# Four early feature tiles ahead of h2's sums, the sums on VectorE, and features loaded into their own tiles

## The chip, the cores and the metric

One Trainium2 chip, one of its cores. The metric is the device time of one launch of the program, in microseconds (us). A time is quoted as the median of several runs; the profile is one execution more.

## The reference, cut to what matters

One layer of a decoder (attention and gated mixers, then a convolutional feed-forward) for 1024 prompt rows and 8 samples of 4 rows, 1056 rows in all, width 1024. What the change touches is the second half:

```python
D_FF = ((8 * D_MODEL // 3) + 127) // 128 * 128        # 2816 = 22 * 128
# ConvFFN: up = (RMSNorm(x)*(1+scale2)+shift2) @ w_up; causal depthwise conv (width 3); gelu(a) * b; @ w_down
# x = x + gate2 * ffn
# Final RMSNorm.
```

`w_up` is 1024 by 5632, so `up` has 44 feature tiles of 128: 22 for `a` and 22 for the gate `b`. All data are fp32.

## The kernel before, in words

Activations lie transposed: partitions are features, columns are the 1056 rows. Every fp32 matmul is made of three: a tensor is split into `hi` (a cast by ScalarE, line 307) and `lo` (the rest, a subtraction by VectorE, line 308), and `mm` (line 56) multiplies hi by hi, hi by lo and lo by hi. A framework orders each engine's queue when the program is built; tags of the buffer pools and explicit calls of `issue_after` bound it.

**The output projection** writes `x1` in three column chunks (`CH`: 384, 384 and 288 columns). `h2`, the normalised and modulated `x1`, is made chunk by chunk behind it (`h2_tile`: a multiplication on VectorE in line 1373, an activation on ScalarE, and for the 32 sample columns a multiplication and an addition, lines 302 and 303, on the engine given by `eng`). The last chunk's are made after the projection has ended.

**The up projection** takes `a` and gate of one feature tile together, a pair, 22 times. A pair is one step of Strassen's scheme in Winograd's form over halves of the 1024 inputs and halves of the rows (`HR` = 528 columns, worked in two `HB` = 264): seven products, each of 24 matmuls of 264 columns. Two of them, `w11` by `BS[0:4]` and `a12` by `BS[4:8]`, need only plain pieces of `h2` from its first 528 columns; the other five need sums of `h2`: `F` (lines 1566 and 1567), `b2 - b1` (1572, on GpSimd), line 1575, each then turned into hi and lo (`turned`: ScalarE in 1555, VectorE in 1556, of which two on GpSimd). They need sums of weights as well, made by GpSimd in lines 1481 to 1484. `first_products` runs the two plain products of pairs 0 and 1 early, while the last chunk of `h2` is made; its result is added into the pair's `up` tile by line 1469. A pair ends with the convolution (ScalarE 1453, VectorE 1454 and 1455), gelu (1537), a multiplication on GpSimd (1538, 1540), and a store of the feature tile to `ff_d` in DRAM (1541). 

**The down projection** goes over the three column chunks again. In the first chunk three outputs run abreast, four features at a time, since the features come back from DRAM as they are needed: `ff_pair` (1603) loads two of them with one transfer into a buffer with the tag "raw", and splits them into their own tiles; `down_weights` loads and splits `w_down` (`weights`, line 1298) through the same three buffers. All weights of the second half of the kernel pass through these "raw" buffers of 128 by 1024. `late` (1591) writes one element of a raw buffer from the last pair's weights until the third output has its first weights, so that the first loads wait for that pair. GpSimd's queue loads `x1` back meanwhile (1663).

The lines that the change touches most:

```python
        raw = late(W([128, 1024], F32, "raw", 3))[:, 0:K * 128]
    ...
            t = slot(F32R) if (k < 6, 6 <= k < 16, k < 6)[c] else R6([128, 768], F32R, "ff", 22)
            split(raw[:, i * w:i * w + w], t[:, 0:w], t[:, 384:384 + w])
```

## Time and profile before

| what | us |
| --- | --- |
| median of 3 runs | 2070.89 (2068.14 to 2075.97) |
| the profiled execution | 2063.98 |
| its span | 2062.3 |
| TensorE busy | 1929.0 (94%) |
| VectorE busy | 1175.0 (57%) |
| ScalarE busy | 811.5 (39%) |
| GpSimd busy | 555.2 (27%) |

The span is what the profile shows from the first to the last instruction; 1.7 us of the execution lie around it. Busy shares are means over the whole span. TensorE idles little, so what a change may bring is found at the places where it idles: in the page's slices, around 1285 to 1345 us (where the up projection begins) and 1755 to 1820 us (where the down projection begins).

### The profile page before, as it was taken

Reading aid. Unit: us, or ns where it says so; the run is one execution under the profiler, and the core shown is the slowest. Engines: PE = TensorE matmul, PEld = TensorE weight load, DVE = VectorE, ACT = ScalarE, POOL = GpSimd, SP = SyncE. Lnnn points to the kernel's source line nnn. Section 1 sums busy time; section 2 is a strip of 40 time slices with the busy share of each in tenths; the row PEclk is TensorE's granted clock in tenths of the full one; section 3 lists DMA queues with packets and bytes.
Section 4 is the critical chain, followed back from the end, with each engine's and each line's share of the span. In section 5 each row is a group of like instructions: output and inputs, shape, how many; then the busy total and the mean of one; then the engine's idle time right before and its main releaser. Section 6 shows DMA issues by size and latency. Waiting matters only on the chain. (4 is left out here: it accounts for less than half of the span.)

```text
span 2062.3 us, 43509 instructions
## 1 busy us (share of the span) xinstructions
PE 1929.0 (94%) x15977; PEld 1748.4 (85%) x15977; DVE 1175.0 (57%) x2697; ACT 811.5 (39%) x1732; POOL 555.2 (27%) x668
## 2 busy tenths in 40 slices
PE   4999999999997999999999999799999999899996
PEld 3899899999995656666679999699999999789986
DVE  6512510121117756667674767988888888555554
ACT  3411211222214645456552355444444444354442
POOL 3310010100001212313320512766565655201010
PEclk7999999999997999999899999899999999999998
DMA  8465577654457666676652645133322222665553
GB/s 313 150 212 161 179 224 248 207 165 158 153 186 223 209 192 207 192 260 181 219 177 89 225 160 174 42 105 104 106 83 85 78 80 84 214 215 185 164 188 97
DMA packets 233620, 345.05 MB, mean 167 GB/s; under 512 B 32544, under 2 KB 183872, under 8 KB 231232
## 3 DMA queue, kind: packets, MB, share of 16 engines
q1 hardware_dynamic: 167008, 245.06, 36.8%
q10 hardware_dynamic: 55312, 58.01, 8.9%
q0 software_dynamic: 11088, 39.21, 5.3%
q8 instruction: 126, 2.06, 0.4%
q14 instruction: 86, 0.70, 0.1%
HBM read 304.91 MB, written 41.43 MB: 168 GB/s over the span
## 5 line engine op out<-in xcount | busy, mean ns | idle before, releaser
L56 PE MATMUL t<-t,t 128*128 128x264 f32 (+10 forms) x15266 | 1848.0, 309 | 96.4 <-ACT t L307 15.5
L56 PEld LDWEIGHTS t<-t,t 128*128 128x128 f32 (+3 forms) x15138 | 1667.3, 170 | 228.4 <-issue 87.3
L308 DVE TENSOR_TENSOR t<-t,t 128x512 fp32r<-128x512 f32 (+5 forms) x544 | 392.8, 736 | 335.1 <-ACT t L307 292.7
L307 ACT CAST t<-t 128x512 fp32r<-128x512 f32 (+5 forms) x544 | 310.4, 588 | 498.0 <-PE t L56 348.0
L1164 POOL TENSOR_SCALAR t<-t,t 128x384 f32<-128x384 f32 (+3 forms) x96 | 119.0, 1253 | 326.9 <-DVE t L1158 100.1
L1139 DVE TENSOR_REDUCE t<-t 128x1 f32<-128x384 f32 (+3 forms) x192 | 96.0, 517 | 56.4 <-PE t L56 55.6
L1513 DVE TENSOR_TENSOR t<-t,t 128x264 f32<-128x264 f32 (+2 forms) x370 | 112.5, 343 | 26.5 <-PE t L56 13.9
L1140 ACT ACTIVATE t<-t,t 128x384 f32<-128x384 f32 (+3 forms) x192 | 105.4, 554 | 54.9 <-DVE t L1139 35.2
L1179 ACT COPY t<-t 128x512 f32<-128x512 f32 (+1 forms) x136 | 76.4, 573 | 65.2 <-PE t L1176 48.9
L1176 PE MATMUL t<-t,t 128*128 128x128 f32 x528 | 87.5, 288 | 0.5 <-ACT t L1179 0.4
L1176 PEld LDWEIGHTS t<-t,t 128*128 128x128 f32 x528 | 57.8, 143 | 24.8 <-issue 23.2
L1624 POOL TENSOR_TENSOR t<-t,t 128x384 f32<-128x384 f32 (+1 forms) x12 | 14.9, 1271 | 234.6 <-ACT t L1681 234.6
L672 ACT ACTIVATE t<-t 128x384 f32<-128x384 f32 (+1 forms) x48 | 22.2, 464 | 136.4 <-PE t L56 105.4
L1454 DVE SCALAR_TENSOR_TENSOR t<-t,t,t 128x1072 f32<-128x1072 f32 x44 | 59.4, 1351 | 17.8 <-ACT t L1453 17.4
L1453 ACT ACTIVATE t<-t,t 128x1072 f32<-128x1072 f32 x44 | 56.6, 1285 | 24.6 <-DVE t L1513 15.5
L674 POOL DMA_DIRECT2D t<-t x16 | 8.5, 532 | 209.5 <-DVE t L673 178.4
L1538 POOL TENSOR_TENSOR t<-t,t 128x1024 f32<-128x1024 f32 x22 | 59.1, 2688 | 15.8 <-ACT t L1537 15.8
L1455 DVE SCALAR_TENSOR_TENSOR t<-t,t,t 128x1072 f32<-128x1072 f32 x44 | 59.3, 1347 | 0.1
L1481 POOL TENSOR_TENSOR t<-t 128x512 f32<-128x512 f32 x22 | 31.6, 1436 | 101.5 <-DMA t<-w_up 63.7
L1329 POOL TENSOR_TENSOR t<-t,t 128x384 f32<-128x384 f32 (+1 forms) x24 | 28.3, 1183 | 96.4 <-DMA t<-t 81.5
L699 POOL TENSOR_TENSOR t<-t,t 128x512 f32<-128x512 f32 (+1 forms) x12 | 11.9, 1002 | 151.6 <-DVE t L690 115.7
L1164 DVE TENSOR_SCALAR t<-t,t 128x384 f32<-128x384 f32 (+3 forms) x96 | 49.8, 571 | 0.9
(280 smaller groups left out, 1166.3 us busy)
## 6 DMA issues: line engine op xcount, KB each, us to landing
t<-psel SPq DMA_DIRECT2D x384, 128.0 KB
t<-pcmp SPq DMA_DIRECT2D x332, 128.0 KB
t<-t POOLq DMA_DIRECT2D x50, 528.0 KB, 4.0
t<-w_up SPq DMA_DIRECT2D x46, 512.0 KB
t<-pcmp ACTq DMA_DIRECT2D x180, 128.0 KB
t<-w_down SPq DMA_DIRECT2D x42, 512.0 KB
t<-psel ACTq DMA_DIRECT2D x128, 128.0 KB
t<-w_ada SPq DMA_DIRECT2D x16, 1024.0 KB
```

The lines of the kernel that those rows point to most:

```text
L56: return pe.matmul(out, lhsT, rhs, start=start, stop=stop)
L307: act.copy(hi, t)
L308: dve.tensor_tensor(lo, t, hi.bitcast(F32), op=OP.subtract)
L1139: dve.tensor_reduce(nm, bk, axis=AX.X, op=OP.max, negate=True)
L1140: act.activation(P[:, w:w + n], bk, AF.Exp, bias=nm, accum_out=s8[:, branch, h, c:c + 1])
L1164: (dve if e == "d" else pool).tensor_scalar(P, P, fc, None, op0=OP.mult)
L1176: pe.transpose(pt[:, 256 * a + 128 * h:256 * a + 128 * h + 128], P[:, c:c + 128], ident)
L1179: act.copy(pp[:, 0:n], pt[:, 0:n])
L1454: dve.scalar_tensor_tensor(acc[:, 0:w], up[:, 1:1 + w], cw[:, n, 1:2], acc[:, 0:w], op0=OP.mult, op1=OP.add)
L1455: dve.scalar_tensor_tensor(acc[:, 0:w], up[:, 2:2 + w], cw[:, n, 2:3], acc[:, 0:w], op0=OP.mult, op1=OP.add)
L1513: dve.tensor_tensor(o, by4(banks[c][:, c0:c0 + n], n), other(c, c0, n) if other else o, op=OP.add)
L1538: pool.tensor_tensor(a[:, 0:NP], a[:, 0:NP], g[:, 0:NP], op=OP.mult)
```

## The change

Four parts.

1. The raw buffers become six of 128 by 512 in place of three of 128 by 1024, each filled by its own transfer of 256 KB, in place of 512 KB.
2. `first_products` runs for four pairs in place of two, in program order between the sums of `h2`. It no longer adds its two products: ScalarE copies both into one tile, and the pair adds them when it starts (line 1499 of the changed kernel). The split of the weights of tiles 2 and 3 comes in here. Pair 0's sums of weights go to other buffers and come after the four.
3. All sums of `h2` are on VectorE: the sample columns, two of the subtractions in `turned`, and `b2 - b1` leave GpSimd.
4. Each feature of the down projection is loaded by its own transfer of 192 KB, for chunks of 384 columns, straight into the `lo` half of the tile that it will have, and split there, through no raw buffer; so three outputs abreast share the raw buffers with nothing. Two pools hold these tiles in place of one (16 and 6 buffers). The condition of `late` is now `not ff[0]`, and as features are asked for before weights, it never holds: no load waits for the last pair any more.

```diff
+    def raw_load(src, late=lambda t: t):
+        t = late(W([128, 512], F32, "raw", 6))[:, 0:src.shape[1]]
+        sync.dma_start(t, src)
+        return t
+
     def weights(src, K, late=lambda t: t):
-        raw = late(W([128, 1024], F32, "raw", 3))[:, 0:K * 128]
-        sync.dma_start(raw, src)
         w = [], []
         for k in range(0, K, 4):
-            hi, lo = parts(raw[:, 128 * k:128 * min(k + 4, K)])
+            hi, lo = parts(raw_load(src[:, 128 * k:128 * min(k + 4, K)], late))
...
     def first_products(j, behind=()):
 
-        up = up_tile()
-        p1 = slot()[:, 0:2 * HB]
-        X = [pA(), pA()]
-        half_products([t[0:4] for t in early[j]], BS[0:4], X, behind[0:1])
-        for c in range(2):
-            act.copy(p1[:, HB * c:HB * c + HB], X[c][:, 0:HB])
-        X = [pU(), pU()]
-        half_products([t[4:8] for t in early[j]], BS[4:8], X, behind[1:])
-        for o, c, c0, n in pieces(up, 0):
-            dve.tensor_tensor(o, X[c][:, c0:c0 + n], p1[:, HB * c:HB * c + n], op=OP.add)
-        return up, p1
+        t = slot()
+        for i, bank in enumerate((pA, pU)):
+            X = [bank(), bank()]
+            half_products([w[4 * i:4 * i + 4] for w in early[j]], BS[4 * i:4 * i + 4], X, behind[i:i + 1] if i == 0 else behind[1:])
+            for c in range(2):
+                act.copy(t[:, HR * i + HB * c:HR * i + HB * c + HB], X[c][:, 0:HB])
+        return t
...
-        r0, r1 = raw_load(A["w_up"][j], 1024), raw_load(A["w_up"][22 + j], 1024)
+        a11, a12, a21, a22 = (raw_load(A["w_up"][n][:, c:c + 512]) for n in (j, 22 + j) for c in (0, 512))
         cst = R5B([128, 2, 16], F32, "cst", 2)
...
-        t0, t1 = slot(), slot()
+        t0, t1 = (R5B([128, RU], F32, "acc", 2) if j == 0 else slot() for _ in range(2))
         s1, s2, s3, s4 = t0[:, 0:512], t0[:, 512:1024], t1[:, 0:512], t1[:, 512:1024]
-        pool.tensor_tensor(s1, a21, a22, op=OP.add)
-        pool.tensor_tensor(s2, s1, a11, op=OP.subtract)
-        pool.tensor_tensor(s3, a11, a21, op=OP.subtract)
-        pool.tensor_tensor(s4, a12, s2, op=OP.subtract)
-        return cst, (a11, a12, a22), (s1, s2, s3, s4)
-
-    def pair(j, cst, raws, sums, begun=None):
+
+        def add_up():
+            pool.tensor_tensor(s1, a21, a22, op=OP.add)
+            pool.tensor_tensor(s2, s1, a11, op=OP.subtract)
+            pool.tensor_tensor(s3, a11, a21, op=OP.subtract)
+            pool.tensor_tensor(s4, a12, s2, op=OP.subtract)
+
+        if j:
+            add_up()
+        return cst, (a11, a12, a22), (s1, s2, s3, s4), add_up
...
-            ua, p1 = begun
+            p1 = begun
+            for o, c, c0, n in pieces(ua, 0):
+                dve.tensor_tensor(o, p1[:, HB * c:HB * c + n], p1[:, HR + HB * c:HR + HB * c + n], op=OP.add)
...
-    begun = [first_products(0, [(1, m1), (0, m1), (1, m2)]), first_products(1, [(0, m2), (0, m2), (0, m2)])]
-    loaded = [pair_weights(0)]
-    for k in range(4):
-        h2_tile(k, *done, eng=pool)
-        h2_tile(4 + k, *done, eng=pool)
+    def sums_of(k):
+        h2_tile(k, *done)
+        h2_tile(4 + k, *done)
         f = slot()
         F.append((f[:, 0:HR], f[:, HR:R]))
         dve.tensor_tensor(F[k][0], b2(4 + k), b2(k), op=OP.subtract)
         dve.tensor_tensor(F[k][1], F[k][0], b1(k), op=OP.add)
         turned(F[k][1], T2[k])
+
+    begun = [first_products(0, [(1, m1), (0, m1), (1, m2)])]
+    sums_of(0)
+    begun.append(first_products(1, [(0, m2), (0, m2), (0, m2)]))
+    sums_of(1)
+    early.append(weights(A["w_up"][2], 8))
+    sums_of(2)
+    begun.append(first_products(2))
+    early.append(weights(A["w_up"][3], 8))
+    sums_of(3)
+    loaded = [pair_weights(0)]
+    begun.append(first_products(3))
+    loaded[0][3]()
     for k in range(4):
-        turned(F[k][0], T3[k], pool if k % 2 else dve)
+        turned(F[k][0], T3[k])
     for k in range(4):
-        pool.tensor_tensor(b2(k), b2(k), b1(k), op=OP.subtract)
+        dve.tensor_tensor(b2(k), b2(k), b1(k), op=OP.subtract)
...
-        if not wd[2]:
+        if not ff[0]:
...
-        (a, b), k = CH[c], len(ff[c])
+        (a, b), k0 = CH[c], len(ff[c])
         w = b - a
-        raw = late(W([128, 1024], F32, "raw", 3))[:, 0:2 * w]
-        sync.dma_start(raw.rearrange("p (k r) -> p k r", r=w), ff_d[k:k + 2, :, a:b].rearrange("k p r -> p k r"))
-        for i in range(2):
-            t = slot(F32R) if (k < 6, 6 <= k < 16, k < 6)[c] else R6([128, 768], F32R, "ff", 22)
-            split(raw[:, i * w:i * w + w], t[:, 0:w], t[:, 384:384 + w])
-            ff[c].append((t[:, 0:w], t[:, 384:384 + w]))
+        for k in (k0, k0 + 1):
+            home = (0 if k < 6 else 1, 2 if k < 6 else 0 if k < 16 else 1, 0 if k < 6 else 1 if k < 16 else 2)[c]
+            t = R6([128, 768], F32R, "ff", 16) if home == 1 else R6B([128, 768], F32R, "ff", 6) if home else slot(F32R)
+            hi, lo = t[:, 0:w], t[:, 384:384 + w]
+            sync.dma_start(lo.bitcast(F32), ff_d[k][:, a:b])
+            split(lo.bitcast(F32), hi, lo)
+            ff[c].append((hi, lo))
```

On GpSimd, where the up projection begins. Before (t_15551 to t_15558 are `h2`, t_16699 to t_16703 the split sums, t_16832 to t_16840 pair 0's weights and their sums):

```order
L302 TENSOR_TENSOR t_15558<-t_15558,t_15523 128x32
L303 TENSOR_TENSOR t_15554<-t_15554,t_262 128x32
L1572 TENSOR_TENSOR t_15551<-t_15551 128x528
L1482 TENSOR_TENSOR t_16839<-t_16839,t_16832 128x512
L1572 TENSOR_TENSOR t_15552<-t_15552 128x528
L303 TENSOR_TENSOR t_15558<-t_15558,t_262 128x32
L1556 TENSOR_TENSOR t_16700<-t_16866,t_16700 128x528
L1572 TENSOR_TENSOR t_15553<-t_15553 128x528
L1484 TENSOR_TENSOR t_16840<-t_16832,t_16839 128x512
L1572 TENSOR_TENSOR t_15554<-t_15554 128x528
L1556 TENSOR_TENSOR t_16702<-t_16892,t_16702 128x528
```

Now, from the last store of `x1` (t_15534) on:

```order
L1390 DMA t_15534<-t_15533 128x288
L1502 COPY t_17135<-t_17021 128x8x2
L1502 COPY t_17139<-t_17021 128x8x2
L1502 COPY t_17344<-t_17335 128x8x2
L1476 TENSOR_TENSOR t_17024<-t_17017,t_17019 128x512
L1478 TENSOR_TENSOR t_17025<-t_17013,t_17017 128x512
L1477 TENSOR_TENSOR t_17024<-t_17024,t_17013 128x512
L1479 TENSOR_TENSOR t_17025<-t_17015,t_17024 128x512
L1476 TENSOR_TENSOR t_17338<-t_17331,t_17333 128x512
```

The sample columns, the differences of 528 columns and the splits are gone; of pair 0 only the four sums of weights stand there, directly followed by pair 1's.

On VectorE, at the same place, behind the last multiplications of `h2`. Before (line 1469 adds an early product, 1566, 1567 and 1575 are sums, 1556 splits):

```order
L1469 TENSOR_TENSOR t_16714<-t_16745,t_16716 128x264
L1566 TENSOR_TENSOR t_16853<-t_15555,t_15551 128x528
L1566 TENSOR_TENSOR t_16866<-t_15556,t_15552 128x528
L1567 TENSOR_TENSOR t_16853<-t_16853,t_15551 128x528
L1567 TENSOR_TENSOR t_16866<-t_16866,t_15552 128x528
L1575 TENSOR_TENSOR t_15555<-t_15555,t_16853 128x528
L1469 TENSOR_TENSOR t_16714<-t_16746,t_16716 128x264
L1566 TENSOR_TENSOR t_16879<-t_15557,t_15553 128x528
L1575 TENSOR_TENSOR t_15556<-t_15556,t_16866 128x528
L1556 TENSOR_TENSOR t_16699<-t_16853,t_16699 128x528
L1469 TENSOR_TENSOR t_16773<-t_16804,t_16775 128x264
L1556 TENSOR_TENSOR t_16695<-t_16853,t_16695 128x528
```

Now (1564, 1565 and 1586 are the sums that stood at 1566, 1567 and 1575; 1583 is `b2 - b1`):

```order
L1564 TENSOR_TENSOR t_16831<-t_15555,t_15551 128x528
L1564 TENSOR_TENSOR t_16901<-t_15556,t_15552 128x528
L1564 TENSOR_TENSOR t_16926<-t_15557,t_15553 128x528
L1565 TENSOR_TENSOR t_16831<-t_16831,t_15551 128x528
L1583 TENSOR_TENSOR t_15551<-t_15551 128x528
L308 TENSOR_TENSOR t_16915<-t_16912,t_16914 128x512
L1565 TENSOR_TENSOR t_16901<-t_16901,t_15552 128x528
L1583 TENSOR_TENSOR t_15552<-t_15552 128x528
L1565 TENSOR_TENSOR t_16926<-t_16926,t_15553 128x528
L1583 TENSOR_TENSOR t_15553<-t_15553 128x528
L1556 TENSOR_TENSOR t_16751<-t_16831,t_16751 128x528
L308 TENSOR_TENSOR t_16991<-t_16988,t_16990 128x512
```

The differences of 1583 and the weight splits of the early tiles 2 and 3 (308) stand between the sums, so the first split of a sum (1556) comes after ten other operations of 512 or 528 columns in place of seven, and the additions of early products have gone to later rows.

On SyncE, whose queue issues the loads, where the last pair's weights end and the down projection's loads begin. Before (t_16713 is `ff_d`; 1410 loads weights of the up projection, 1603 two features, 1298 weights of the down projection):

```order
L1410 DMA t_22423<-w_up 128x1024
L1410 DMA t_22425<-w_up 128x1024
L1603 DMA t_22691<-t_16713 128x2x384
L1603 DMA t_22700<-t_16713 128x2x384
L1298 DMA t_22709<-w_down 128x512
L1298 DMA t_22716<-w_down 128x512
L1298 DMA t_22723<-w_down 128x512
L1603 DMA t_22785<-t_16713 128x2x384
L1603 DMA t_22793<-t_16713 128x2x384
L1298 DMA t_22801<-w_down 128x512
```

Now (1298 loads all weights, 1617 one feature of `ff_d`, t_16765):

```order
L1298 DMA t_22583<-w_up 128x512
L1617 DMA t_22849<-t_16765 128x384
L1617 DMA t_22853<-t_16765 128x384
L1617 DMA t_22857<-t_16765 128x384
L1617 DMA t_22861<-t_16765 128x384
L1298 DMA t_22865<-w_down 128x512
L1298 DMA t_22871<-w_down 128x512
L1617 DMA t_22941<-t_16765 128x384
L1617 DMA t_22945<-t_16765 128x384
L1298 DMA t_22877<-w_down 128x512
L1298 DMA t_22957<-w_down 128x512
L1298 DMA t_22963<-w_down 128x512
```

Features go out in fours and twos, weights in twos and fives, and a feature load names its own tile and no raw buffer.

## Rows read from the trace of the kernel before

**Rows 1.** Busy time by stretch: stretch, length, then each engine's busy time (instructions): PE, PEld, DVE, ACT, POOL; clock; DMA.

```profile
1284.80:1390.00 105.20, 88.06 (x667) 85.17 (x667) 95.03 (x159) 47.38 (x75) 75.59 (x86) 0.94 0.20 68
1400.00:1740.00 340.00, 340.00 (x2795) 340.00 (x2794) 284.83 (x522) 139.07 (x201) 209.37 (x261) 1.00 0.26 88
1756.40:1821.00 64.60, 51.08 (x250) 48.42 (x249) 32.12 (x61) 26.56 (x50) 8.22 (x12) 0.87 0.69 237
1821.00:1861.00 40.00, 40.00 (x232) 40.00 (x231) 24.07 (x44) 20.45 (x39) 0.00 (x0) 1.00 0.60 186
```

**Rows 2.** What TensorE waited for, 1284.8 to 1390: total us, times, longest.

```profile
PE t L56 <- POOL t L1556: 5.2, 1, 5.2
PE t L56 <- DVE t L1469: 4.8, 2, 3.1
PE t L56 <- DVE t L1556: 3.5, 3, 3.0
```

**Rows 3.** Groups on GpSimd, 1284.8 to 1371: count | busy us, mean ns | idle before.

```profile
L1572 POOL TENSOR_TENSOR t<-t 128x528 f32<-128x528 f32 x4 | 12.5, 3134 | 4.0 <-DVE t L1566 4.0
L1481 POOL TENSOR_TENSOR t<-t 128x512 f32<-128x512 f32 x4 | 6.9, 1733 | 8.9 <-DVE t L1528 3.6 <-issue 2.6 <-DMA t<-w_up 2.6
```

**Rows 4.** Groups on VectorE by form, 1284.9 to 1304.6.

```profile
L1556 DVE TENSOR_TENSOR t<-t,t 128x528 fp32r<-128x528 f32 x4 | 5.8, 1478 | 0.0
...
L1373 DVE TENSOR_TENSOR t<-t,t 128x288 f32<-128x288 f32 x8 | 3.0, 449 | 0.7 <-PE t L282 0.7
```

**Rows 5.** Timeline of GpSimd and VectorE, 1307 to 1313: start, us, line, instructions in the run.

```profile
1307.61 7.23 POOL L1572 TENSOR_TENSOR t<-t 128x528 f32<-128x528 f32 x1 [4.04 <-DVE t L1566]
...
1309.28 3.18 DVE L1556 TENSOR_TENSOR t<-t,t 128x528 fp32r<-128x528 f32 x5
```

**Rows 6.** Groups on VectorE by form, 1400 to 1740.

```profile
L308 DVE TENSOR_TENSOR t<-t,t 128x512 fp32r<-128x512 f32 x116 | 108.5, 936 | 6.6 <-ACT t L307 2.7
...
L1513 DVE TENSOR_TENSOR t<-t,t 128x32 f32<-128x32 f32 x83 | 14.9, 180 | 0.0
```

**Rows 7.** The page's costliest groups, whole span.

```profile
L1513 DVE TENSOR_TENSOR t<-t,t 128x264 f32<-128x264 f32 (+2 forms) x370 | 112.5, 343 | 26.5 <-PE t L56 13.9
...
L1454 DVE SCALAR_TENSOR_TENSOR t<-t,t,t 128x1072 f32<-128x1072 f32 x44 | 59.4, 1351 | 17.8 <-ACT t L1453 17.4
...
L1538 POOL TENSOR_TENSOR t<-t,t 128x1024 f32<-128x1024 f32 x22 | 59.1, 2688 | 15.8 <-ACT t L1537 15.8
```

**Rows 8.** What TensorE waited for, 1756.4 to 1821.

```profile
PE t L56 <- ACT t L307: 12.0, 4, 5.5
PE t L56 <- DVE t L308: 1.6, 2, 1.3
```

**Rows 9.** Timeline of ScalarE, 1756 to 1822: in brackets the idle time before, and what ended it.

```profile
1757.57 1.29 ACT L1453 ACTIVATE t<-t,t 128x1072 f32<-128x1072 f32 x1 [1.66 <-issue]
...
1804.34 0.93 ACT L307 CAST t<-t 128x384 fp32r<-128x384 f32 x2 [3.12 <-DMA t<-t]
```

**Rows 10.** What the queue of SyncE waited for, 1740 to 1830.

```profile
SPq L1298 <- DVE t L308: 25.9, 19, 3.4
SPq L1603 <- DVE t L308: 19.9, 10, 4.1
...
SPq L1298 <- DVE t L1591: 7.4, 2, 4.2
```

**Rows 11.** Transfers, 1757 to 1810: rate in 40 slices; an issue's count, KB, us to landing.

```profile
GB/s 375 238 167 0 182 42 270 0 80 402 370 249 193 58 344 306 101 0 196 222 296 396 430 402 376 289 2 122 317 155 92 22 145 213 402 432 414 425 414 400
DMA packets 5950, 12.64 MB, mean 238 GB/s; under 512 B 550, under 2 KB 3050, under 8 KB 5948
...
t<-t POOLq DMA_DIRECT2D x9, 528.0 KB, 7.2
```

**Rows 12.** The chain that ended last, around the start of the down projection: start, us, what.

```profile
1757.17 2.94 DMA t<-w_down
...
1763.42 3.04 DMA t<-t
```

## What I predict, and how

> **What bounds the kernel now.** The page first: TensorE is busy 94% of the span, so a gain must come from where it idles, and the page's slices name two places. The table of stretches gives them their size. In the steady part of the up projection TensorE works without a gap, 2795 matmuls in 340.00 us, or 0.1216 us for one of 264 columns; in the down projection 232 in 40.00 us, or 0.1724 us for one of 384 [rows 1]. At these rates the 667 matmuls from 1284.8 to 1390 would take 81.1 us of the 105.2: the entry of the up projection loses 24.1 us. The 250 from 1756.4 to 1821 would take 43.1 us of 64.6: the entry of the down projection loses 21.5 us. Part of each loss is no wait. TensorE is busy 88.06 and 51.08 us, 7.0 and 8.0 us more than these rates need, and the granted clock means 0.94 and 0.87 there, against 1.00 in the steady parts: columns done at 1.2 in place of 2.4 GHz. A wait that goes takes its slow columns with it. The rest of the span is left alone.
>
> **What TensorE waits for at the first entry.** 5.2 us for a split on GpSimd (line 1556), 4.8 for VectorE's early additions (1469), 3.5 for its splits (1556) [rows 2]. The two engines slow each other. A split of 528 columns means 1.48 us on VectorE from 1284.9 to 1304.6 [rows 4], where GpSimd worked nearly without a gap; five in a row took 3.18 us, 0.64 each, at 1309 [rows 5]. In that time one difference on GpSimd (line 1572) lasted 7.23 us [rows 5], while the other three took (12.5 - 7.23) / 3 = 1.76 [rows 3]. So when one goes at its own pace the other is held up, and the last sums of GpSimd came late. Moving the sums costs VectorE instructions and gives back pace.
>
> **The entry, step by step.** In the changed order VectorE has, from the last chunk's first multiplication to pair 0's last addition, 48 operations of 512 or 528 columns, 8 of 288, 16 additions of 264 or 232, and 22 of 32 columns or fewer. At the free pace: 48 x 0.64 = 30.7 us [rows 5]; the 8 multiplications 3.0 us [rows 4]; 16 x 0.34 = 5.4 [rows 7]; 22 x 0.18 = 4.0 [rows 6]. Sum 43.1 us. GpSimd still has sums of weights there: eight, for two pairs, x 1.73 us [rows 3] = 14 us. Beside GpSimd a split means 0.94 us where GpSimd is busy 209 of 340 us [rows 1, 6], so 0.30 us of a 0.64 us operation is lost at 62% cover: some 0.45 us for each us of GpSimd. That makes 6 us. For waits on TensorE and ScalarE I add 2 us, a choice. Pair 0 then ends at 1284.9 + 51.1 = 1336.0.
>
> Pairs 1 to 3 have their two plain products behind them: five products, 120 matmuls, 14.6 us of TensorE. VectorE needs 284.83 x 20.43 / 340 = 17.1 us a pair [rows 1] (20.43 us are 168 matmuls), less the two splits of 0.94 that such a pair no longer has [rows 6]: 15.2 us. VectorE sets the pace, by little, and pair 3 ends at 1336.0 + 3 x 15.2 = 1381.6. By then TensorE has done 192 + 4 x 120 = 672 matmuls; before, it had done 667 at 1390.0. Gain 8.4 + 5 x 0.12 = **9 us**. From pair 4 on TensorE is the bound again, as before.
>
> Bounds: if GpSimd costs VectorE nothing there and waits add nothing, 8 us more, 17. If every long operation goes at the steady pace of 0.94, 14.4 in place of the 6 us: 8.4 less, 0.6. TensorE's own floor, 672 x 0.1216 = 81.7 us, allows no more than 24.
>
> ScalarE takes 8 more copies of 264 columns; it is busy 47 of 105 us there [rows 1], and the copies' results are wanted a pair later. The four weight splits of tiles 2 and 3 are in the 48, as are the differences and splits that leave GpSimd.
>
> **The entry of the down projection.** TensorE waits 12.0 us for casts and 1.6 for subtractions [rows 8]; ScalarE in turn waits for loads, up to 3.12 us at one cast [rows 9]. The loads are late because they are issued late: SyncE's queue waited 25.9 us with weights and 19.9 us with features until a subtraction had emptied a raw buffer, and 7.4 us for the gate of line 1591 [rows 10]. The chain shows the ring: load of 2.94 us, split, next load of 3.04 us, split [rows 12]. The transfers themselves are not the limit: the mean was 238 GB/s, with slices at nothing beside slices above 400 [rows 11].
>
> After the change a feature's load waits for no raw buffer, six weight buffers are the weights' own, and the gate is gone: 4 features and 2 weights stand next behind the last pair's loads, then 2 features and 5 weights, most of which can land while TensorE finishes the pair (the steady part moves 88 GB/s [rows 1]). What stays: tiles that lie where the sums of h2 lay can be loaded only once the last products have read those, and the last feature. Its convolution starts 1.2 us after TensorE's last product of the pair [rows 9], the steps from there to its return take some 18 us: 1.29 us on ScalarE and as much for gelu [rows 9], twice 1.35 on VectorE, 2.69 on GpSimd [rows 7], a store of 7.2 [rows 11], a load of 3.04 [rows 12]. It is wanted after 180 matmuls of the abreast part, 31 us, so it has some 11 us to spare. In the new order casts of earlier features stand ahead of that convolution and take part of these 11 us. I leave 4 us of the 21.5 in place: gain **17.5 us**. Bounds: only the first cast and subtraction wait, 1.5 us left, gain 20; half of the loss stays, gain 10.
>
> One load per feature in place of one for two costs SyncE 11 more issues in the first chunk. The rows speak for little: 384 KB landed in 3.04 us, 256 KB in 2.94 [rows 12], so nearly all of it is a fixed time that loads in flight share. The Trainium skill says otherwise of small loads: DMA: Bandwidth & Descriptors, in its section on measured bandwidth, wants transfers of 1 MiB or more for 75% of the peak, and in Anatomy of one DMA (the path through GpSimd) fits 2.0 us plus the bytes at 436 GB/s. By that fit, an estimate for another path, a feature takes 2.45 us, and sixteen one after another 39 us against the 34 us that the abreast part has, so 5 us more would stay and the sum be 21.5. The slices above 400 GB/s, reached with loads of 256 and 384 KB, do not agree with a rate that the size of a load alone decides.
>
> Other edges: the loads of w_out and of the later outputs are halved too, where TensorE waits little; I take nothing.
>
> **The sum.** 9 + 17.5 = 26.5 us. The profiled execution took 2063.98 us, so 2037.5; it lay 6.9 us under the median of the runs, so I forecast **2044 us** for the median. With the ends of both bounds the gain is 10.6 to 37 us: 2034 to 2060.
>
> **Rivals.**
> A. VectorE takes it all back: by the order it has nine long and 16 short operations more (8.6 us at the free pace) and the early additions still to make, so pair 3 ends no earlier, and only the down projection gains. For it: VectorE is busy 95 of 105 us there [rows 1]. Against: its long operations were slow beside GpSimd, and reached 0.64 us when GpSimd was held up. 2063.98 - 17.5 + 6.9 = 2053.
> B. Loads bind in the first down chunk. Of the features, 6 to 21 can be loaded only from about the end of the last pair on, and the abreast part's 198 matmuls take 34 us. If each load takes its 2.94 us [rows 12] by itself, as in the ring before, that is 47 us: 13 us more stay, gain 9 + 4.5 = 13.5, time 2057. Against it: loads in flight shared the queue above 400 GB/s [rows 11], and no feature waits for a buffer any more. The Trainium skill's rule on small transfers, above, points this way.
> C. Slower. The long operations on VectorE keep the pace of 1.48 us [rows 4] although GpSimd has left, because the cause was another (the last stores, TensorE's own reads). Then 48 x 1.48 + 12.4 + 2 = 85.4 us to pair 0's end, 34 us more than forecast: the entry loses 25.3, the down projection gains 17.5: 2063.98 + 7.8 + 6.9 = 2079. It decides from 48 x (p - 0.64) = 6 + 26.5 on, p = 1.32 us. The five at 0.64 speak against it: VectorE does reach that pace here.
> D. No net effect. The last feature is late: casts of features that wait for their own loads hold up the last pair's convolution on ScalarE by more than the 11 us of room, say 17 us late, 6 us of waiting; with the lower bounds of both other gains (0.6 and 10), 0.6 + 10 - 6 = 4.6, time 2066.
>
> **How the numbers follow.** Forecast 0.60, A 0.14, B 0.10, C 0.06, D 0.10. The forecast's bounds, 2034 to 2060, take in A and B, 0.84 together; below they are stretched by 3 us, as far as the fastest run lies under the median, so 2031 to 2060. A change of 0.5% is 10.4 us, about what this kernel's runs can tell from none. Faster by that: nearly all of the forecast, and most of A and B, 0.80. Within: D and the rest of A, 0.13. Slower: C and a little of D, 0.07.
>
> **What would show it.** Right: no sum of h2 on GpSimd, splits of 528 columns at 0.6 to 0.9 us, one wait of TensorE of 5 to 10 us ahead of the product with T2 in place of four, pairs 1 to 3 paced by VectorE at about 15 us; at the down projection features loading before TensorE ends the last pair, SyncE without the 45 us of waits for subtractions, TensorE's waits under 6 us. Wrong: long operations above 1.3 us with GpSimd idle; casts in the first down chunk that still wait 2 to 3 us each for a load; a long wait for the last feature.

## The result, and the profile after

The changed kernel takes 2051.7 us (median of 5 runs, 2046.84 to 2054.31) against 2069.05 us of the kernel before (5 runs): 0.9911 of its time, 95% interval 0.9888 to 0.9934. That is 17 us faster where 26.5 were forecast. 2051.7 lies in the range of 2031 to 2060, and close to the 2053 of rival A.

The profiled execution has a span of 2049.9 us, 12.4 less than before. Three lengths tell where they come from. The matmuls of 288 columns of the output projection's last chunk, and all up to the last row statistics, take the same time in both traces, so their start is a mark:

```profile
1257.03 5.27 PE L56 MATMUL t<-t,t 128*128 128x288 f32 x38
```

```profile
1261.06 5.27 PE L56 MATMUL t<-t,t 128*128 128x288 f32 x38
```

These are rows of TensorE's timeline, of the kernel before first, then of the changed one. The changed kernel is 4.0 us late there. The time of this mark differs from one execution to the next: in the 14 profiles of this document it lies between 1257.03 and 1268.37, and that of the kernel before is the earliest. I count the **up projection** from 27.25 us after this mark (the start of the last statistics' broadcast in both) to the first matmul of 384 columns of the down projection, and the **down projection** from there to the end of the span. All runs below are read so.

| | mark | up projection | down projection | span |
| --- | --- | --- | --- | --- |
| before | 1257.03 | 471.7 | 306.3 | 2062.3 |
| changed | 1261.06 | 475.0 | 286.6 | 2049.9 |
| forecast | | -9 | -17.5 | |
| measured | +4.0 | +3.3 | -19.7 | -12.4 |

In this table a minus is time saved. The down projection gained what was forecast and a little more. The up projection, forecast 9 us shorter, got 3 us longer. Busy time by stretch, the changed kernel (columns as in [rows 1]):

```profile
1288.80:1394.00 105.20, 88.25 (x677) 86.66 (x677) 95.24 (x180) 47.45 (x83) 64.07 (x58) 0.92 0.24 78
1390.00:1450.00 60.00, 57.36 (x457) 56.94 (x456) 54.86 (x82) 23.38 (x34) 42.53 (x53) 0.97 0.29 99
1450.00:1700.00 250.00, 250.00 (x2057) 249.99 (x2056) 243.41 (x390) 102.27 (x147) 178.04 (x188) 1.00 0.28 89
1763.30:1828.00 64.70, 61.69 (x345) 61.03 (x345) 44.72 (x85) 36.73 (x72) 9.23 (x14) 0.97 0.81 278
```

The first row answers to the first of [rows 1], 4.0 us later: 677 matmuls in place of 667 in 105.2 us, 1.2 us gained and not 9. In the second TensorE, which had no gap there before, idles 2.6 us. In the last it is busy 61.7 of 64.7 us, where it was 51.1 of 64.6.

What TensorE waited for, the changed kernel from 1230 to 1400 (total us, times, longest); it answers to [rows 2]:

```profile
PE t L56 <- ACT t L307: 10.5, 2, 10.2
PE t L56 <- DVE t L1513: 5.7, 3, 4.4
```

The waits of before are gone, and one of 10.2 us has come, for a cast, from 1306.9 to 1317.1. Its cause stands in the timelines of GpSimd, VectorE and ScalarE at that time (start, us, line, tiles; in brackets the idle time before):

```profile
1300.98 13.03 POOL L1476 TENSOR_TENSOR t<-t,t 128x512 f32<-128x512 f32 x1 [11.24 <-DMA t<-w_up]
1313.97 1.25 POOL L1478 TENSOR_TENSOR t<-t,t 128x512 f32<-128x512 f32 x1
1315.19 1.25 POOL L1477 TENSOR_TENSOR t<-t,t 128x512 f32<-128x512 f32 x1
```

```profile
1310.31 0.72 DVE L1565 TENSOR_TENSOR t<-t,t 128x528 f32<-128x528 f32 x1
...
1312.17 0.72 DVE L1583 TENSOR_TENSOR t<-t 128x528 f32<-128x528 f32 x1
1317.13 1.21 DVE L308 TENSOR_TENSOR t<-t,t 128x512 fp32r<-128x512 f32 x1 [4.24 <-ACT t L307]
```

```profile
1316.47 1.14 ACT L307 CAST t<-t 128x512 fp32r<-128x512 f32 x2 [12.05 <-POOL t L1477]
```

GpSimd's first sum of pair 0's weights (line 1476) lasts 13.03 us and ends 1.1 us after VectorE has run out of work at 1312.9; the next two take 1.25 us each. ScalarE's cast of `s2`, made by line 1477, waits for them, TensorE waits for the cast, and VectorE for the casts behind it. Not all of the 10.2 us is GpSimd's: the product that waits needs four sums of `h2` too, and VectorE makes the fourth (line 1565) only at 1310.31, 3.4 us after TensorE has stopped. From 1294 to 1313 VectorE itself ran at the forecast pace, or nearly:

```profile
L1556 DVE TENSOR_TENSOR t<-t,t 128x528 fp32r<-128x528 f32 x10 | 6.7, 716 | 0.0
```

(VectorE by form; the mean is of records that overlap a little: the starts lie 0.62 us apart.) From 1340 to 1400, in pairs 0 to 3, VectorE's groups show the opposite:

```profile
L308 DVE TENSOR_TENSOR t<-t,t 128x512 fp32r<-128x512 f32 x18 | 16.0, 889 | 0.0
L1453 DVE SCALAR_TENSOR_TENSOR t<-t,t,t 128x1072 f32<-128x1072 f32 x7 | 14.5, 2068 | 0.0
L1452 DVE SCALAR_TENSOR_TENSOR t<-t,t,t 128x1072 f32<-128x1072 f32 x7 | 10.7, 1536 | 3.8 <-ACT t L1451 3.8
...
L1499 DVE TENSOR_TENSOR t<-t 128x264 f32<-128x264 f32 x4 | 5.5, 1417 | 0.0
```

The convolution's two operations (lines 1452 and 1453, which stood at 1454 and 1455) take 1.54 and 2.07 us in the mean, against 1.35 for each over the whole span before ([rows 7] has the first), and the addition of early products (line 1499) takes 1.42 us, where the same line took 0.44 between 1293 and 1311. Here VectorE is the slow one.

In the down projection, the same view of TensorE's waits from 1763 to 1828; it answers to [rows 8]:

```profile
PE t L56 <- DVE t L1344: 2.8, 1, 2.8
```

The 13.6 us of waits for casts and subtractions of loaded data are gone. SyncE's queue, though, from 1740 to 1830, answering to [rows 10]:

```profile
SPq L1298 <- DVE t L308: 48.1, 30, 8.5
```

It waits as long for subtractions as it did, only with weights and further ahead of the need. The transfers from 1764 to 1817:

```profile
DMA packets 8434, 15.83 MB, mean 299 GB/s; under 512 B 946, under 2 KB 4869, under 8 KB 8429
```

They moved 299 GB/s where they had moved 238 [rows 11], with features of 192 KB in place of pairs of 384.

### The profile page after: what moved, and what is told of

The parts are those of the page before. It is cut to its first block, busy times and chain, and to the rows that moved or that the text cites. A ratio compares the mean times of both kernels' runs of the same rounds, so it can differ in the third digit from the quotient of the medians.

```text
span 2049.9 us, 43955 instructions
## 1 busy us (share of the span) xinstructions
PE 1922.9 (94%) x15977; PEld 1745.8 (85%) x15977; DVE 1216.9 (59%) x2694; ACT 812.7 (40%) x1740; POOL 573.5 (28%) x646
## 4 chain that ended last, share of the span: by engine, by line
PE 77%; DVE 8%; DMA 7%; issue 3%; ACT 3%; POOL 1%; SPq 1%; ACTq 0%; DVEq 0%; POOLq 0%
PE t L56 73%; PE t L1176 3%; DMA t<-pcmp 2%; DMA t<-t 1%; DMA t<-psel 1%; DVE t L308 1%; DMA t<-xT 1%; DVE t L1513 1%; ACT t L307 1%; PE t L993 1%; POOL t L1476 1%; DVE t L1164 1%; DVE t L1139 1%; SPq L513 1%; DVE t L871 0%
## 5 line engine op out<-in xcount | busy, mean ns | idle before, releaser
L308 DVE TENSOR_TENSOR t<-t,t 128x512 fp32r<-128x512 f32 (+2 forms) x478 | 387.7, 818 | 320.8 <-ACT t L307 316.0
L1513 DVE TENSOR_TENSOR t<-t,t 128x264 f32<-128x264 f32 (+2 forms) x366 | 107.0, 339 | 2.0 <-PE t L56 2.0
L1453 DVE SCALAR_TENSOR_TENSOR t<-t,t,t 128x1072 f32<-128x1072 f32 x44 | 78.3, 1780 | 0.0
L1452 DVE SCALAR_TENSOR_TENSOR t<-t,t,t 128x1072 f32<-128x1072 f32 x44 | 72.9, 1656 | 8.2 <-ACT t L1451 7.2
L1476 POOL TENSOR_TENSOR t<-t,t 128x512 f32<-128x512 f32 x22 | 48.7, 2213 | 94.1 <-DMA t<-w_up 82.9
L1538 POOL TENSOR_TENSOR t<-t,t 128x1024 f32<-128x1024 f32 x22 | 53.3, 2423 | 20.1 <-ACT t L1537 20.1
```

What stands on the lines that cost most here:

```text
L308: dve.tensor_tensor(lo, t, hi.bitcast(F32), op=OP.subtract)
L1452: dve.scalar_tensor_tensor(acc[:, 0:w], up[:, 1:1 + w], cw[:, n, 1:2], acc[:, 0:w], op0=OP.mult, op1=OP.add)
L1453: dve.scalar_tensor_tensor(acc[:, 0:w], up[:, 2:2 + w], cw[:, n, 2:3], acc[:, 0:w], op0=OP.mult, op1=OP.add)
L1476: pool.tensor_tensor(s1, a21, a22, op=OP.add)
L1513: dve.tensor_tensor(o, by4(banks[c][:, c0:c0 + n], n), other(c, c0, n) if other else o, op=OP.add)
```

## The experiments

Three theories come from these traces. **1**: the entry is lost to pair 0's sums of weights, held up on GpSimd by VectorE's dense run. **2**: VectorE is the bound from pair 0 to pair 4 whatever the waits are called (rival A), and takes back what the early tiles gain. **3**: the smaller loads spoil the entry. Medians and ratios are against runs of the kernel before in the same session; lengths come from one profile each. `entry_only` and `raw_large`, whose up projections are the same code, gave 471.3 and 472.8, so I read no less than 2 us from a length of the up projection. The down projection of the changed kernel, the same code in nine of these profiles, lasted 283.8 to 288.5, so there I read no less than 5. By "lead" I mean how much sooner than in the kernel before TensorE starts the same matmul of 264 columns, counted from the first and timed from the mark.

| run | median us | ratio to before, 95% interval | up | down |
| --- | --- | --- | --- | --- |
| changed kernel | 2051.7 | 0.9911 (0.9888 to 0.9934) | 475.0 | 286.6 |
| down_only | 2055.2 | 0.9928 (0.9899 to 0.9957) | 477.1 | 286.1 |
| entry_only | 2074.3 | 1.0014 (0.9996 to 1.0032) | 471.3 | 312.1 |
| sums0_vector | 2047.3 | 0.9876 (0.9843 to 0.9908) | 471.3 | 285.3 |
| raw_large | 2059.6 | 0.9941 (0.9921 to 0.9961) | 472.8 | 297.2 |
| conv_left_out | 2036.7 | 0.9842 (0.9815 to 0.9868) | 462.3 | 283.8 |
| two_tiles | 2052.5 | 0.9912 (0.9886 to 0.9937) | 471.6 | 286.1 |
| sums_gpsimd | 2047.1 | 0.9880 (0.9851 to 0.9908) | 469.4 | 287.2 |
| gate_first_sums0 | 2054.7 | 0.9927 (0.9901 to 0.9953) | 479.7 | 285.9 |
| gate_back | 2053.0 | 0.9911 (0.9879 to 0.9944) | 474.6 | 289.7 |
| gpsimd_sums0_vector | 2044.7 | 0.9877 (0.9852 to 0.9902) | 467.7 | 288.5 |
| large_halves_gpsimd | 2049.3 | 0.9907 (0.9882 to 0.9933) | 471.8 | 285.6 |
| sums04_vector | 2045.3 | 0.9868 (0.9843 to 0.9894) | 467.0 | 288.3 |

**down_only**: the changed kernel with `first_products`, the sums of `h2` and pair 0's sums of weights as before. The cut is against the kernel before.

```diff
-        r0, r1 = raw_load(A["w_up"][j], 1024), raw_load(A["w_up"][22 + j], 1024)
+        a11, a12, a21, a22 = (raw_load(A["w_up"][n][:, c:c + 512]) for n in (j, 22 + j) for c in (0, 512))
...
-        raw = late(W([128, 1024], F32, "raw", 3))[:, 0:2 * w]
...
+            sync.dma_start(lo.bitcast(F32), ff_d[k][:, a:b])
```

> Parts 1 and 4 alone (smaller raw buffers, features loaded into their tiles, gate gone); the entry of the up projection is that of the kernel before. If the whole gain comes from the down projection, the up projection lasts 472 us as before, the down projection 287 as in the changed kernel, and the time is some 20 us under before, about 2049, a little faster than the changed kernel. If the smaller buffers alter the entry, or if the down projection gained because the pairs ahead of it were different, the down projection lasts over 295 and the time is above 2057.

The down projection is 286.1, as in the changed kernel: its gain is its own and owes nothing to the entry. But the up projection is 477.1, 5.3 over the kernel before, whose entry it shares. So the buffers do reach into the up projection, and the median is 15 us under before and not 20.

**entry_only**: the kernel before with four early tiles and the sums on VectorE, large buffers. The cut is against the kernel before.

```diff
-    begun = [first_products(0, [(1, m1), (0, m1), (1, m2)]), first_products(1, [(0, m2), (0, m2), (0, m2)])]
+    begun = [first_products(0, [(1, m1), (0, m1), (1, m2)])]
+    sums_of(0)
...
-        pool.tensor_tensor(b2(k), b2(k), b1(k), op=OP.subtract)
+        dve.tensor_tensor(b2(k), b2(k), b1(k), op=OP.subtract)
```

> Parts 2 and 3 alone (four early tiles, sums on VectorE); raw buffers and down projection are those of the kernel before. If the entry costs 3 us as the two traces say, the up projection lasts 475 us, the down projection 306, and the time is 2072, 3 us over before. If the loss of the entry in the changed kernel came from the smaller raw buffers (the weights of pair 0 loaded later), the up projection lasts 463 here, as predicted, and the time is 2060.

Up projection 471.3, no change from 471.7, and the wait of 10.2 us is there too. The new entry by itself is worth nothing: its lead is 6.9 us at the end of pair 0 (312 matmuls) and 0.2 by the 1300th. Neither of the two expected values came: the change neither costs 3 us by itself nor gains 9 with the large buffers. Its down projection of 312.1 is 6 over that of before with the same code for it, which I can't explain: the order of what precedes it is another.

**sums0_vector**: the four sums of pair 0's weights on VectorE.

```diff
-        def add_up():
-            pool.tensor_tensor(s1, a21, a22, op=OP.add)
+        def add_up(eng=pool):
+            eng.tensor_tensor(s1, a21, a22, op=OP.add)
...
-    loaded[0][3]()
+    loaded[0][3](dve)
```

> The changed kernel with the four sums of pair 0's weights on VectorE in place of GpSimd. Theory 1: GpSimd's first sum lasts 13 us because VectorE's dense run holds it up, and TensorE waits 10 us for it; on VectorE the four sums take 2.6 us, so this wait falls to under 3 us, the up projection lasts 463 to 467 and the time is 2042. Theory 2: VectorE has too much work there in any case, the wait only changes its name (for a split of line 1556 or an addition), the up projection lasts 473 to 478 and the time is 2050 to 2054.

The result lies between the two. TensorE's waits from 1230 to 1460 in its trace:

```profile
PE t L56 <- DVE t L1513: 10.1, 6, 3.5
PE t L56 <- ACT t L307: 7.1, 3, 5.1
```

The wait for the cast falls from 10.2 to 5.1 us at most, and the waits for VectorE's additions (1513) rise to 10.1. The up projection gains 3.7 us of the 8 to 12 that theory 1 had. At the end of pair 0 the lead is 13.1 us, 6.6 more than the changed kernel's 6.5; by the 900th matmul it is 0.4 against -2.7. So the wait was real, and about half of what it gave back went into later ones.

**raw_large**: the changed kernel with the raw buffers and loads of before; features still go straight to their tiles.

```diff
-        t = late(W([128, 512], F32, "raw", 6))[:, 0:src.shape[1]]
-        sync.dma_start(t, src)
+        raw = late(W([128, 1024], F32, "raw", 3))[:, 0:K * 128]
+        sync.dma_start(raw, src)
```

> The changed kernel with the three large raw buffers of before, one load of 512 KB for eight blocks; features still go straight into their tiles. If the gain of the down projection is that features need no raw buffer and the gate is gone, the down projection stays under 290 us. If the six small buffers are what keeps the weights' loads ahead, the down projection lasts 295 to 300, and the time is 2058 to 2063. On the entry: theory 3, that pair 0's sums are late because its weights land late (GpSimd waited 11 us for them), gives another length than 475 here if the ring of large buffers loads them at another time.

The down projection takes 297.2: of its 19.7 us, 10.6 are the six buffers and 9.1 what is left, the features' own loads and the missing gate. The entry is hardly other than with small buffers (472.8), and TensorE's 10.2 us wait is still there, so theory 3 does not explain it.

**conv_left_out**: leaves out the two VectorE operations of the convolution for the first five pairs.

```diff
+        if n % 22 > 4:
+            dve.scalar_tensor_tensor(acc[:, 0:w], up[:, 1:1 + w], cw[:, n, 1:2], acc[:, 0:w], op0=OP.mult, op1=OP.add)
```

> The changed kernel, but the two VectorE operations of the convolution are left out for the first five pairs (20 operations of 1.33 us and more; the features of these pairs are then not what the reference has). Theory 2, VectorE sets the pace from pair 0 to pair 4 and so takes back what the early tiles gain: the waits of TensorE for VectorE's additions (8 us up to pair 5) go, and the up projection lasts 464 to 468 us in place of 475. Theory 1, only the 10 us wait for pair 0's sums of weights counts: that wait lies ahead of the first convolution and stays, and the up projection lasts 473 to 475.

Up projection 462.3, 12.6 less, more than theory 2 expected, and the wait of 10.2 us is still in the trace:

```profile
PE t L56 <- ACT t L307: 10.2, 1, 10.2
```

After it TensorE waits less than 2 us more up to 1460; in this kernel the stretch that had 457 matmuls has 496:

```profile
1390.00:1450.00 60.00, 60.00 (x496) 60.00 (x495) 51.49 (x85) 23.38 (x34) 34.95 (x44) 1.00 0.30 99
```

This bears theory 2 out: VectorE's work in pairs 0 to 4 sets the end. With that work lifted the lead is 7.0 us at the end of pair 0, 9.1 at the end of pair 3 and 9.4 at the end of the up projection, where the changed kernel's goes from 6.5 over 1.3 to -3.3. (The kernel before had 495 matmuls in the stretch that answers to this one.)

**two_tiles**: two early tiles, sums on VectorE.

```diff
-    early.append(weights(A["w_up"][2], 8))
     sums_of(2)
-    begun.append(first_products(2))
```

> The changed kernel with first_products for two tiles again, the sums still on VectorE. If VectorE is the bound up to pair 4, the two plain products more or less ahead of the sums make no difference at the end: up projection 473 to 477 us. If the four tiles are what gains and the sums on VectorE what loses, it lasts 480 or more.

The median is 2052.5, that of the changed kernel. The length says 471.6, 3.4 us shorter and under what was expected; length and median don't agree here (in this profile the mark lies at 1268.37, 4.8 us later than in any other). By either, tiles 2 and 3 gain nothing in the changed kernel.

**sums_gpsimd**: four early tiles, sums of `h2` on GpSimd as before.

```diff
-        h2_tile(k, *done)
-        h2_tile(4 + k, *done)
+        h2_tile(k, *done, eng=pool)
+        h2_tile(4 + k, *done, eng=pool)
...
-        dve.tensor_tensor(b2(k), b2(k), b1(k), op=OP.subtract)
+        pool.tensor_tensor(b2(k), b2(k), b1(k), op=OP.subtract)
```

> The changed kernel with the sums of h2 on GpSimd as in the kernel before, four early tiles kept. If the sums on VectorE are worth something (they end its slow pace beside GpSimd), the up projection gets longer than 475 us, 478 to 484. If they are what made VectorE the bound, it lasts 466 to 471.

The up projection takes 469.4: moving the sums to VectorE cost the up projection 5.5 us. With VectorE the bound, GpSimd's slow sums were the cheaper place.

**gate_first_sums0**: as sums0_vector, each pair's loads in another order.

```diff
-        a11, a12, a21, a22 = (raw_load(A["w_up"][n][:, c:c + 512]) for n in (j, 22 + j) for c in (0, 512))
+        a21, a22, a11, a12 = (raw_load(A["w_up"][n][:, c:c + 512]) for n in (22 + j, j) for c in (0, 512))
```

> The changed kernel with pair 0's sums of weights on VectorE, as in the run above, and with the loads of each pair in another order: the gate's two blocks, which the first sum needs, ahead of the other two. If the smaller raw buffers cost because the sums of weights wait for a pair's last load and then fall beside VectorE's splits and convolution, VectorE's busy time from 1450 to 1700 us falls from 244 towards the 211 of the large buffers, and the up projection lasts 466 to 469 us, the time is 2043. If the load order does not matter, 471 us and 2047 as in the run above.

Neither value came: 479.7. TensorE now waits for VectorE's additions in the middle of the stage too (7.4 us after 1450), and its lead, still 5.0 us at the 1000th matmul, is -4.3 at the 2000th, though VectorE is less busy there (231 of 250 us).

**gate_back**: the gate of the first loads again.

```diff
-        if not ff[0]:
+        if not wd[2]:
```

> The changed kernel with the gate back (the first loads of the down projection wait for the last pair's weights, as before). If the down projection gains because its first loads no longer wait for the last pair, it lasts 290 to 296 us in place of 286.6, and the time is 2055 to 2061. If the gate cost nothing beside the buffers, 285 to 288 and 2050 to 2054.

The down projection takes 289.7, 3.1 us more than in the changed kernel. That is less than the 5 us that I read from this length, and the median, 2053.0, can't tell the two apart. So how the 9.1 us divide between the gate and the features' own loads is not shown.

**gpsimd_sums0_vector**: both edits that helped, sums_gpsimd and sums0_vector.

> The changed kernel with the sums of h2 on GpSimd, as before the change, and the four sums of pair 0's weights on VectorE: both of the edits that helped alone. If VectorE's load up to pair 4 is the bound, moving the sums of h2 off it helps here too: up projection 464 to 468 us, time 2044. If the two edits heal the same wait, no more than either alone: 469 to 472 us, 2047.

The up projection takes 467.7, the first case, at its upper end, and this is the shortest median of all full kernels, 2044.7. Against the changed kernel that is 7 us, but the two intervals overlap by a little.

**large_halves_gpsimd**: as sums_gpsimd, with large buffers, in the down projection one load in each half.

```diff
+            if not halves:
+                t = W([128, 1024], F32, "raw", 3)
+                halves.extend([t[:, 0:512], t[:, 512:1024]])
+            t = halves.pop(0)[:, 0:128 * (e - k)]
```

> The changed kernel with the sums of h2 on GpSimd, and with the three large raw buffers kept: one load for eight blocks in the up projection, and in the down projection each large buffer holds two loads of 256 KB in its halves. If the small loads cost the up projection because GpSimd's sums then fall beside VectorE's work, VectorE's busy time from 1450 to 1700 us is 211 and the up projection lasts 465 to 468 us. The down projection lasts 287 to 290 if it is the number of loads in flight that counts, 295 to 298 if a buffer must come free for each load. Time 2045 to 2048 in the first case, 2053 to 2057 in the second.

The down projection holds its 285.6, so there it is the number of loads under way that counts and not how the buffers are cut. The other half fell. VectorE's busy time from 1450 to 1700 is 210.05 us as expected, against 243.41 in the changed kernel, and the up projection is no shorter for it (471.8 against 469.4).

**sums04_vector**: as gpsimd_sums0_vector, pairs 1 to 4's sums of weights on VectorE too.

```diff
-            add_up()
+            add_up(dve if j < 5 else pool)
```

> The kernel of the run before last (sums of h2 on GpSimd, pair 0's sums of weights on VectorE) with the sums of weights of pairs 1 to 4 on VectorE as well: four operations a pair, 2.6 us at VectorE's free pace, in place of some 6 us on GpSimd. Theory A: what slows VectorE in pairs 1 to 4 is GpSimd beside it (0.45 us for each us, 2.7 us a pair); then the move costs about what it gives back, its long operations get faster, and the up projection lasts 464 to 468 us against 467.7. Theory B: VectorE has simply too many operations up to pair 4, whatever GpSimd does; then 10 us more work there makes the up projection longer, 473 to 478 us.

The up projection takes 467.0, as theory A has it. VectorE has 16 more long operations and is no later. Its splits of 512 columns from 1340 to 1400 take 0.77 us (first row), against 1.25 in gpsimd_sums0_vector, with these sums on GpSimd (second row):

```profile
L308 DVE TENSOR_TENSOR t<-t,t 128x512 fp32r<-128x512 f32 x18 | 13.8, 766 | 0.0
```

```profile
L308 DVE TENSOR_TENSOR t<-t,t 128x512 fp32r<-128x512 f32 x18 | 22.5, 1251 | 0.0
```

## Why the prediction was right and wrong

**What bounds the kernel**: the two places were right, and the rest of the span did not move by more than executions differ.

**The entry** failed, in three steps of its working.

*The count.* "By then TensorE has done 192 + 4 x 120 = 672 matmuls; before, it had done 667 at 1390.0" sets side by side two counts that do not start together. In both traces 24 matmuls of the first plain product run before [rows 1] begin (in the kernel before from 1279.38 to 1284.2). The 672 include them and the 667 do not. By 1390.0 the kernel before had done 690, so the forecast's own times give 8.4 - 18 x 0.12 = 6.2 us and not 9.

*Pair 0.* "GpSimd still has sums of weights there: eight ... That makes 6 us" took the two engines' conflict to cost VectorE alone. In the trace of the changed kernel it went the other way at first: VectorE kept 0.62 us for each operation, GpSimd's first sum lasted 13.03, and TensorE waited 10.2 us, where 5 to 10 were forecast, for a sum of four that the forecast had treated as off the path. From the last chunk's first multiplication to pair 0's last addition:

```profile
1289.59:1342.06 52.47, 40.60 (x306) 39.62 (x306) 43.80 (x95) 27.34 (x57) 27.76 (x15) 0.87 0.17 56
```

VectorE is busy 43.8 us there, near the 43.1 of the free pace, and idle 8.7. The forecast had 49.1 and 2. The one term is 5.3 us too large and the other 6.7 too small, so pair 0 ends about when it was to end (1342.06, or 1338.0 less the late start, against 1336.0), by luck. The row that showed the hold-up was at hand, the 7.23 us difference of [rows 5]; I read it as a reason to move sums off GpSimd and did not ask what would happen to the sums that stay there. The Trainium skill has a rule for this (SBUF — State Buffer, section Who interferes with whom): a VectorE operation with two inputs in SBUF contends with a GpSimd instruction that reads SBUF, the ports that they share are an exclusive lock, and the order of issue decides who blocks. The trace agrees that one of the two is held up; a hold over some twenty VectorE operations in a row, 12 us, is more than those sentences would lead one to expect.

*The pace.* "VectorE needs ... 15.2 us" for each of pairs 1 to 3. The last additions of pairs 0 and 3 end at 1342.06 and 1391.94, 16.6 us a pair; the last convolution operations, which fall behind the additions, start at 1350.59 and 1406.81, 18.7 us a pair. The 15.2 came from the steady stretch, where VectorE idles 55 of 340 us and part of GpSimd's work falls into these gaps. A VectorE that is behind has few gaps (it is busy 52.2 of the 56.2 us between those convolutions), so more of GpSimd's work lies beside its own, and its long operations take the times shown above. sums04_vector is the run that shows that the work beside it is what slows it, and conv_left_out that VectorE decides the end. That the steady stretch was one with large buffers is no explanation: entry_only and raw_large keep them, and a pair takes 20.0 and 20.1 us there by the convolutions. Nor did the loss end with these pairs: "From pair 4 on TensorE is the bound again" was too early, as VectorE's convolutions were still behind.

The lead shows the steps: 6.7 us at the 216th matmul (the 192 of the plain products and one product more), 6.5 at the end of pair 0, 1.3 at the end of pair 3 (672), -2.7 at the 900th and -3.4 at the 1300th. Of the 12.3 us by which this gain was missed, 2.8 are the count, some 4.9 the time up to the end of pair 3, and some 4.7 what was lost after it. The lower bound for this gain, 0.6, was too high for the same reasons.

**The down projection**: right, 19.7 for 17.5, near the upper bound of 20. The mechanism was right in its outcome and half right in its parts. The six small buffers, of which the forecast said little, are 10.6 us of it (raw_large); the features' own loads and the missing gate are the other 9.1 together, and which of the two gives how much is not shown. "What would show it" had SyncE's waits for subtractions gone; they stayed as long (48.1 us) and moved to weights that are needed later. The last feature was no problem, as forecast: its convolution started at 1768.8, 5.5 us after the last product, and TensorE waited for no load.

**Rivals.** A came about: pair 3 ends only 1.3 us earlier, the next pairs later, and only the down projection gains; 2053 forecast for it, 2051.7 measured. I gave it 0.14 for VectorE's 95 of 105 busy us and argued against it by the free pace, which held only until the sums were done. B did not come about: TensorE waited for no load in the first down chunk, and 299 GB/s were moved. C did not come about: the sums of h2 ran at 0.62 us. VectorE was slow again one stage later, but beside GpSimd, and C needs another cause. D did not come about: the last feature was not late.

**The sum**: the up projection misses its forecast by 9 + 3.3 = 12.3 us and the down projection gives 2.2 more than its own, so 16.4 of the 26.5 us are left, beside 17.4 between the medians. (The spans differ by 12.4, since the changed kernel's profile reaches the mark 4.0 us late.) That 2051.7 lies in the range is owed to its width, which was drawn to take in rival A, and not to the mechanism forecast for the entry.

**What stays open**: how the cut of the raw buffers acts on the up projection. Small ones cost it 5.3 us with the old entry (down_only), 2.2 with the new (raw_large), and gain 2.4 with the sums on GpSimd (large_halves_gpsimd), each from one profile; the last two are hardly more than two profiles of the same code differ by, so the change of sign is not shown. In every kernel with small ones VectorE is busy 243 to 244 of 250 us in the steady part (1450 to 1700), or 231 with the other load order, and in every one with large ones 210 or 211. Where it is 243 or 244 TensorE still works without a gap to speak of (249.6 to 250.0 us); why the small loads keep VectorE busy longer was not found.

## What to carry to other kernels

Before moving work off one of two engines that slow each other, list what stays on it, ask who waits for that, and price the conflict in both directions. An engine that is 84% busy in the steady state has little room to catch up after a late start: take its pace there from a stretch in which it has no gaps, not from the mean. When two counts of work are compared, start both at the same mark. Where loads wait for a buffer and not for bandwidth, more of them under way through more buffers gain, even with smaller loads.

## What the runs showed of the hardware that I had not expected

GpSimd can be held up by VectorE for as long as VectorE has work without a gap: one sum of 512 columns, 1.25 us when alone, lasted 13.03 us beside operations that started 0.62 us apart, and 12.13 and 12.12 us in entry_only and raw_large. In other stretches the loss lies with VectorE: an addition of 264 columns from SBUF took 1.42 us in the mean, against 0.42 for those of the same size that read PSUM (line 1513) in the same 60 us:

```profile
L1513 DVE TENSOR_TENSOR t<-t,t 128x264 f32<-128x264 f32 x17 | 6.9, 422 | 0.0
```

What decides which of the two loses was not settled by any run here.
